# Squares of one half summed on GpSimd, a pair of x splits moved by two steps, and new step times in a hybrid attention trunk

## The chip, the cores and the metric

One core of a Trainium2 chip runs the whole kernel. The time is the device time of one execution in microseconds (us); lower is better. The kernel before takes 2347.12 us, the median of three runs (2345.92 to 2347.37). The profile is of one further execution.

## What is computed

One layer over 1024 positions of width 2048 (`x`, f32). Two groups of eight heads share one input projection; each has q, k, v and a gate.

```python
hn = rmsnorm(h, norm_mix_g);  proj = hn @ w_in          # sb_q..sb_g, df_q..df_g
sb_out = stick_breaking_attention(sb_q, sb_k, sb_v)      # 8 heads of 128
df_out = differential_attention(rope(df_q), rope(df_k), df_v, lam)   # 8 heads, (softmax1 - lam*softmax2) @ v
df_out = rmsnorm(df_out, subln_g) * (1 - lambda_init)
mixed  = concat([sb_out * silu(sb_g), df_out * silu(df_g)])
h = h + mixed @ w_out
gate = sigmoid(rmsnorm(h, norm_ple_g) @ w_ple_gate)
h = h + gate * (p @ w_ple_proj)
return rmsnorm(h, norm_final_g)
```

## The kernel before

Everything lies with the 2048 columns on the partitions (16 tiles of 128) and 512 positions, one half, along the free dimension. A product in f32 is made of three fast ones: each operand is split into a rounded high part (ScalarE, `A.copy` or `A.activation`) and the rest as low part (VectorE, a subtraction), and TensorE does high*high, high*low and low*high. So each operand tile needs a load, a cast on ScalarE and a subtraction on VectorE before TensorE can use it.

The stages, in the order of time in the profile:

1. 0 to 620 us: v and gate columns, with a seven-product (Strassen) scheme, class `Seven`, lines L713 to L715.
2. 620 to 1626 us: 32 units, one for each half and head. A unit (`unit`, L263 to L265) makes q and k of one head from the 16 x tiles in four pieces `pc` of 24 matmuls; beside it the attention of the heads before is interleaved. Half 1 comes first (heads 8 to 15, differential, then 0 to 7, stick-breaking), then half 0 in the same order of heads.
3. 1626 to 1965 us: output projection, again `Seven`. In phase 0 (`ph` 0) six products of each of eight blocks `u` are made for partial results; in phase 1 seven products of 12 matmuls each (A11, A22 of the block before, S2, S4 of the block before, A12, S1, S3) finish a block: four tiles of h, two of each half. `put` stores each tile, and `row_squares` adds its squares to the sum for the next norm.
4. 1965 to 2343 us: gate product, embedding, final norm. `norm` (L2013) turns the sum of squares into the row's scale by a matmul with a matrix of ones.

What sets the order. The five engines run their queues in the order in which the program wrote them; an instruction that waits holds up all behind it on its engine. `Side` is a clock in ticks: one tick for each three matmuls of a unit. A step is entered with a time in ticks, and the instructions are written when the tick comes; fractions only order steps within one tick. The tables at the top of the file are these times: `SC`, `TT` and so on for the differential heads (scores, transposes of the weights), `SBB`, `SBS`, `SBT`, `SGAP` for the stick-breaking ones. `SGAP[0]`, 3.5, is the distance in ticks from `turn` (L484: transposes, then the split L502 on ScalarE and L507 on VectorE) to `mix` (L527 to L532: weights times v) in half 0. Index 0 of a table is half 0, index 1 half 1.

The seam is where unit 15 (half 1, head 7) gives way to unit 16 (half 0, head 8). The x tiles of half 1 are replaced by those of half 0. The last eight come late: `late_x0` loads one (L1352, `xl<-h_d`) and writes its split, `xh` on ScalarE (L1355) and `xl` on VectorE (L1356), `4 + 3 * i` ticks later. In the same ticks VectorE takes q and k of head 7 out of PSUM (L1611), ScalarE casts them (L1619) and VectorE makes their low parts (L1614); the scores of head 7 (L341 to L343) need them.

In phase 1 of the projection the weights of the next blocks are loaded, combined and split while the products run: `diff` (L769) makes T1 to T4 on VectorE from the four loaded blocks, and each load of a next block (L760, `wraw<-w_out`) is issued when the difference that last reads the old block is written, block 21 after T4. `whigh` (L804) casts on ScalarE, `wlow` (L818) subtracts on VectorE. `sums` (L1847 on ScalarE, L1848 to L1856 on VectorE) combines the tiles of h for the gate product. TensorE may add A22 onto the PSUM tile of S3 only when VectorE has read it (L1968, `u3`).

`row_squares` takes the two halves apart. For half 1 ScalarE squares into one buffer, `spare32`, shown as `masks` (L1435), and GpSimd adds it to `total` (L1436). For half 0 ScalarE squares into one of two tiles in turn, `rsq` (L1428), and GpSimd issues a DMA that adds it to one of two tiles in HBM, `sq_d` (L1429; the first two are plain stores). Both `sq_d` tiles are loaded again in the gate stage (L2163), and `norm(*sums0)` makes two matmuls with ones. As one of the `rsq` tiles lies where `cs` lay, the ring of weight buffers of the projection leaves `cs` out: nine buffers in place of ten.

Of the kernel before, what the change touches and what calls it, by code (L numbers as in the profile page):

```python
# [31 lines left out]
EPS = 1e-6  # L32
SUB_EPS = 1e-5

SC = ((6.5, 7, 9.0, 11.5, 15.5, 17.5, 20.0, 21.5), (10.5, 10.5, 15.5, 23.0))
TT = ((19, 31, 16.0), (21.5, 36.5, 20))
DGAP = (3, 7.0)
DF0 = (0.5, 1, 1.5, 3.5, 5.5)
DF1 = (1, 1.0, 3, 5, 6.5)
LV = ((3.0, 4.0), (1, 2))  # L40
LT = ((1, 1.5), (0.5, 2.0))
LM = ((0.5, 2.0, 4, 5), (1.5, 2.5, 4.5, 6.5))
LN = ((1, 6.0), (1, 4.5))
PRIO = 300
NORM_LAT = ((8.0, 8.5), (13, 11))
XLAT = 5
SBB = ((20, 20, 15, 15.5, 16, 16.5, 16.5, 16.0), (19.5, 8.5, 5.0, 3.5, 4.0, 5.5, 5.0, 3.0))
SBS = ((0.5, 3.5, 15.5, 23.5), (-2.5, 3, 7.0, 13.0))
SBT = ((15, 31, 13), (16.0, 30.0, 14.5))
SGAP = (3.5, 6.0)  # L50
SBL = ((1.5, 3, 6.0), (1, 2, 8.0))
SVG = ((18, 37.5, 40, 40, 46), (30.5, 37.5, 41.0, 43.5, 49.5))
CST = (16.5, 19.5)
ROPE = ((-0.4, 1.5, 3.0, 4.0, 2.2, 4.5, 6.0, 7.0), (-1.9, -1, 0, 1, 0.20000000000000018, 2, 3, 4))
ROPE_ = ((3.5, 4.0, 6.0, 10.0, 11.6, 12.5, 15.0), (6.5, 7, 9.5, 12.5, 12.6, 13.5, 14))
VGD = ((19.5, 37, 37.0, 39.5, 44.0), (22.5, 32.5, 35.5, 37.0, 45.0))
LAM0 = 0.8 - 0.6 * math.exp(0.0)
NEG = -1.0e30
EXTRA = 5, 9
PIECES = 30  # L60
LOWG = ORDER1[H - 1:H + 1]
LAST = ((2.5, 3.5), (2, 4.0))
X1T = 1, 2.5, 4, 5.5, 9, 10.5, 12, 13.5
VLAG = 3

# [6 lines left out]
def _body(ctx, nc, tc, ap):  # L72
# [174 lines left out]
    side = Side()  # L247
# [380 lines left out]
    with tc.tile_pool(name="at", bufs=2) as at, ExitStack() as banks:  # L628
# [739 lines left out]
        sq_d = dram.tile([2, P, HALF], F32, name="sq_d", tag="sq_d")  # L1368
        SUMS = "S1", "S2", "S3", "S4"

        def load_operand(ph, nm, i, eng=nc.sync):
# [18 lines left out]
        ssh = {}  # L1390
# [26 lines left out]
        spare32 = masks.bitcast(F32)[:, 0:HALF]  # L1417
        totals = {}

        nsq = [0]  # L1420

        def row_squares(hf, o):
            if hf == 0:
                if nsq[0] % 2:
                    t = at.tile([P, 2, HALF], F32, name="rsq", tag="cs", bufs=1)[:, 0, :]
                else:
                    t = ev.tile([P, HALF], F32, name="rsq", tag="rstd0", bufs=1)
                A.activation(t, o, AF.Square)  # L1428
                G.dma_start(sq_d[nsq[0] % 2], t, **(dict(accum_op=ALU.add) if nsq[0] > 1 else {}))  # L1429
                nsq[0] += 1  # L1430
            elif not totals:
                totals[1] = ev.tile([P, HALF], F32, name="total", tag="rstd1", bufs=1)
                A.activation(totals[1], o, AF.Square)
            else:
                A.activation(spare32, o, AF.Square)  # L1435
                G.tensor_tensor(totals[1], totals[1], spare32, op=ALU.add)  # L1436

        def put(o, ph, hf, ch):

# [80 lines left out]
        for half in (1, 0):  # L1520
# [5 lines left out]
            for hd in (ORDER0, ORDER1)[half]:  # L1526
# [27 lines left out]
                if half == 1 and hd == ORDER1[-1]:  # L1554
                    def late_x0(kt, wait):
                        with tc.issue_after(lastw[0].ins):
                            side.add([(wait, load_x0(kt))])

                    def swap(pc):
                        for i, kt in enumerate((pc * 2, pc * 2 + 8, pc * 2 + 1, pc * 2 + 9)):  # L1560
                            if pc < 2:
                                side.add([(1 + 4 * i, load_x0(kt))])
                            else:
                                side.add([(1 + i, partial(late_x0, kt, 4 + 3 * i))])

                    side.add([(8 * pc + 7, partial(swap, pc)) for pc in range(4)])

# [585 lines left out]
        for u in range(8):  # L2153
            p6(u + 1)
            if u == 0:
                p5(1)
            plew_load(u + 2, 1)
            load_hc(u + 9)
            if u == 5:
                sums0 = [ev.tile([P, HALF], F32, name="sums", tag=t, bufs=1) for t in ("rstd0", "ssq")]  # L2160
                for i, t in enumerate(sums0):
                    with tc.issue_after(op.loaded.ins):
                        nc.sync.dma_start(t, sq_d[i])  # L2163
            if u == 6:
                gate_loads("S3", 0)
            if u == 7:
                embedding_load(0, "xt")
                plew_load(0, 1)
                plew_load(0, 0)
            p3(u)  # L2170
            if u < 7:
                plew(u + 1, 1)
                if u:
                    p5(u + 1)
            if u == 6:
                norm(*sums0)
                ssh[0] = sums0[0]


        hpair = {}  # L2180
# [302 lines left out]
```

## Time and profile before

| | before |
|---|---|
| median of 3 runs | 2347.12 us (2345.92 to 2347.37) |
| the profiled execution, its time | 2344.73 us |
| its span, first to last instruction | 2342.9 us |
| granted TensorE clock, mean | 0.996 |
| TensorE busy | 2300.4 us (98%) |
| VectorE busy | 1828.0 us (78%) |
| ScalarE busy | 1170.5 us (50%) |
| GpSimd busy | 345.4 us (15%) |
| 16 DMA engines, mean rate | 248 GB/s |

How to read it. TensorE works nearly all the time, and the change leaves it almost the same matmuls, so the time can only move by what TensorE waits, by the clock that it is granted, and by the matmuls that go. The view of waits names, for each line, whom it waited for: the sum, how often, and the longest. A timeline row has the start, the duration, and in brackets the idle time of the engine before it and what ended it. The chain of waits goes back from the end of a stretch, at each step to what released it. In the view by stretches the column PEclk is the granted clock. The profiled execution took 2344.73 us, 2.39 us less than the median of the runs.

### The profile page before, as it was taken

The page shows a single profiled execution, that of the slowest core. Times are in us where ns is not written, and L with a number is a line of the kernel's source. Part 1 is how long each engine was busy: PE and PEld are TensorE (multiplying, and loading weights), DVE is VectorE, ACT ScalarE, POOL GpSimd, SP SyncE. Part 2 cuts the span into 40 slices and gives each one's busy share as a digit, 9 for nine tenths or more (in the row PEclk, how much of TensorE's full clock was granted, in tenths as well). Part 3 has the DMA queues.
Part 4 walks back from the last instruction along what each step waited for, and adds up shares of the span by engine and source line. Part 5 has one row for each costly group of instructions (what it writes and reads, how often), then busy time and mean ns, then how long its engine had stood idle before and what let it go on. Part 6 is the DMA issues. An engine that isn't in the chain of part 4 may idle for free.

```text
span 2342.9 us, 32443 instructions
## 1 busy us (share of the span) xinstructions
PE 2300.4 (98%) x10976; PEld 1916.2 (82%) x10976; DVE 1828.0 (78%) x3181; ACT 1170.5 (50%) x2184; POOL 345.4 (15%) x486
## 2 busy tenths in 40 slices
PE   9999999999999999999999999999999999999997
PEld 7888888888888878887888888888888877888886
DVE  7699786777678877777888876668887887788788
ACT  6334243333267776445677765445633335533544
POOL 1211112223200030000001101101111232000000
PEclk9999999999999999999999999999999999999998
DMA  7699579999977788787756666678888778898666
GB/s 254 225 307 354 175 240 288 293 279 265 310 252 252 256 269 314 262 259 245 223 176 189 194 202 208 201 215 244 211 220 217 227 227 278 277 336 290 239 230 218
DMA packets 266549, 581.01 MB, mean 248 GB/s; under 512 B 30032, under 2 KB 58960, under 8 KB 266384
## 3 DMA queue, kind: packets, MB, share of 16 engines
q1 hardware_dynamic: 191776, 394.35, 49.8%
q0 software_dynamic: 55312, 149.71, 24.4%
q10 hardware_dynamic: 19296, 34.90, 4.3%
q8 instruction: 86, 1.41, 0.2%
q14 instruction: 79, 0.65, 0.1%
HBM read 373.32 MB, written 213.91 MB: 251 GB/s over the span
## 4 chain that ended last, share of the span: by engine, by line
PE 76%; DMA 10%; DVE 8%; ACT 4%; issue 1%; SPq 0%; ACTq 0%; DVEq 0%
PE acc L265 8%; PE acc L263 8%; PE acc L264 8%; PE pbc L713 6%; PE pbc L715 6%; PE pbc L714 6%; DMA wlo<-wlo_d 3%; PE pa L714 2%; PE pa L713 2%; PE pa L715 2%; PE tp L484 2%; DMA wraw<-w_gate 2%; DMA wraw<-w_out 2%; PE pb L715 1%; PE pb L713 1%
## 5 line engine op out<-in xcount | busy, mean ns | idle before, releaser
L804 ACT CAST wpr<-T 128x512 fp32r<-128x512 f32 x208 | 125.1, 621 | 484.2 <-DVE T L769 391.6
L263 PE MATMUL acc<-xh,whi 128*128 128x512 f32 x768 | 312.5, 407 | 0.0
L265 PE MATMUL acc<-xh,wlo 128*128 128x512 f32 x768 | 302.0, 393 | 4.7 <-DMA wlo<-wlo_d 4.7
L264 PE MATMUL acc<-xl,whi 128*128 128x512 f32 x768 | 300.9, 392 | 0.0
L265 PEld LDWEIGHTS acc<-xh,wlo 128*128 128x128 f32 x768 | 144.6, 188 | 40.3 <-DMA wlo<-wlo_d 8.5
L264 PEld LDWEIGHTS acc<-xl,whi 128*128 128x128 f32 x768 | 145.4, 189 | 23.7
L263 PEld LDWEIGHTS acc<-xh,whi 128*128 128x128 f32 x768 | 144.9, 189 | 23.6 <-DVE qk L1611 0.3
L804 ACT CAST wpr<-wraw 128x512 fp32r<-128x512 f32 x144 | 88.3, 617 | 140.5 <-DMA wraw<-tw_d 31.3
L818 DVE TENSOR_TENSOR wpr<-T,wpr 128x512 fp32r<-128x512 f32 x208 | 142.5, 685 | 4.7 <-ACT wpr L804 2.1
L946 POOL DMA_DIRECT2D vg_d<-hc x120 | 88.6, 770 | 287.9 <-DVE hc L943 128.9
L502 ACT CAST awh<-tp 128x256 fp32r<-128x256 f32 (+1 forms) x160 | 80.5, 503 | 80.4 <-PE tp L484 74.8
L507 DVE TENSOR_TENSOR awl<-tp,awh 128x256 fp32r<-128x256 f32 (+1 forms) x160 | 92.4, 577 | 35.1 <-ACT awh L502 34.6
L713 PE MATMUL pbc<-cS,wpr 128*128 128x512 f32 x288 | 112.0, 389 | 0.0
L714 PE MATMUL pbc<-cS,wpr 128*128 128x512 f32 x288 | 112.0, 389 | 0.0
L715 PE MATMUL pbc<-cS,wpr 128*128 128x512 f32 x288 | 112.0, 389 | 0.0
L326 DVE CUSTOM_DVE_ANT_0 z<-z,masks 128x512 f32<-128x512 f32 (+7 forms) x128 | 96.9, 767 | 19.0 <-PE z L346 9.8
L818 DVE TENSOR_TENSOR wpr<-wraw,wpr 128x512 fp32r<-128x512 f32 x144 | 97.2, 682 | 11.3 <-ACT wpr L804 11.3
L378 DVE TENSOR_TENSOR_SCAN st<-pt 128x511 f32<-128x511 f32 (+3 forms) x64 | 86.7, 1354 | 23.5 <-ACT pt L371 22.5
L371 ACT ACTIVATE pt<-z 128x512 f32<-128x512 f32 (+3 forms) x64 | 41.7, 652 | 77.3 <-DVE z L354 75.4
L532 PE MATMUL av<-awl,v 128*128 128x256 f32 x256 | 73.0, 285 | 1.2 <-DVE awl L507 1.2
L530 PE MATMUL av<-awh,v 128*128 128x256 f32 x256 | 72.0, 281 | 0.7 <-ACT awh L502 0.7
L531 PE MATMUL av<-awh,v 128*128 128x256 f32 x256 | 72.4, 283 | 0.0
(596 smaller groups left out, 6833.7 us busy)
## 6 DMA issues: line engine op xcount, KB each, us to landing
wlo<-wlo_d SPq DMA_DIRECT2D x94, 512.0 KB, 5.2
whi<-whi_d SPq DMA_DIRECT2D x74, 512.0 KB, 4.1
wraw<-w_vg SPq DMA_DIRECT2D x129, 256.0 KB, 4.2
vg_d<-hc POOLq DMA_DIRECT2D x120, 256.0 KB, 5.5
wraw<-w_in SPq DMA_DIRECT2D x54, 512.0 KB, 5.0
wraw<-w_gate SPq DMA_DIRECT2D x92, 256.0 KB, 5.1
wraw<-w_out SPq DMA_DIRECT2D x72, 256.0 KB, 4.6
wlo_d<-wlo SPq DMA_DIRECT2D x34, 512.0 KB, 3.4
```

What stands on the lines that cost most here:

```text
L263: T.matmul(acc[c], hi[:, k2, kh, c, :], xh, start=first, stop=False)
L264: T.matmul(acc[c], hi[:, k2, kh, c, :], xl, start=False, stop=False)
L265: T.matmul(acc[c], lo[:, k2, kh, c, :], xh, start=False, stop=last)
L326: V.tensor_tensor_reduce(z, z, mwide[:, 0:n], -DF_SCALE, 3.0e38, ALU.add, ALU.min, mx)
L378: V.tensor_tensor_scan(st[:, off + 1:nkey], pt[:, off:nkey - 1], pt[:, off:nkey - 1], initial=1.0, op0=ALU.mult, op1=ALU.bypass)
L507: V.tensor_tensor(wl[:, o, :], tp[:, o, :], wh[:, o, :].bitcast(F32), op=ALU.subtract)
L713: T.matmul(o, wh[:, w], xh, start=start and k == 0, stop=False, skip_group_check=True)
L714: T.matmul(o, wh[:, w], xl, start=False, stop=False, skip_group_check=True)
L715: T.matmul(o, wl[:, w], xh, start=False, stop=k == 3, skip_group_check=True)
L804: A.copy(t[:, 0], src)
L818: V.tensor_tensor(t[:, 1], src, t[:, 0].bitcast(F32), op=ALU.subtract)
L946: G.dma_start(vg_d[hf, blk, u], o, **(dict(accum_op=ALU.add) if ph else {}))
```

## The change

Four things are changed.

The squares of half 0 now go the way of half 1: ScalarE squares into the one buffer `spare32`, GpSimd adds into `totals[0]`. `sq_d`, its 16 storing DMAs and its two loads go, and `norm` gets one tile. The ring of weight buffers of the projection and of the gate stage behind it has `cs` again, ten buffers. `late_x0` writes its splits `6 + 3 * i` ticks after the load instead of `4 + 3 * i`. Some 25 numbers of the tables are others; no step is added or taken away by them.

```diff
-SGAP = (3.5, 6.0)
+SGAP = (4.0, 6.0)
...
 def row_squares(hf, o):
-    if hf == 0:
-        if nsq[0] % 2:
-            t = at.tile([P, 2, HALF], F32, name="rsq", tag="cs", bufs=1)[:, 0, :]
-        else:
-            t = ev.tile([P, HALF], F32, name="rsq", tag="rstd0", bufs=1)
-        A.activation(t, o, AF.Square)
-        G.dma_start(sq_d[nsq[0] % 2], t, **(dict(accum_op=ALU.add) if nsq[0] > 1 else {}))
-        nsq[0] += 1
-    elif not totals:
-        totals[1] = ev.tile([P, HALF], F32, name="total", tag="rstd1", bufs=1)
-        A.activation(totals[1], o, AF.Square)
+    if hf not in totals:
+        totals[hf] = ev.tile([P, HALF], F32, name="total", tag=f"rstd{hf}", bufs=1)
+        A.activation(totals[hf], o, AF.Square)
     else:
         A.activation(spare32, o, AF.Square)
-        G.tensor_tensor(totals[1], totals[1], spare32, op=ALU.add)
+        G.tensor_tensor(totals[hf], totals[hf], spare32, op=ALU.add)
...
-op.ring = [e for e in WRING if e != ("at", "cs")]
...
-                                side.add([(1 + i, partial(late_x0, kt, 4 + 3 * i))])
+                                side.add([(1 + i, partial(late_x0, kt, (6 if pc == 2 else 6) + 3 * i))])
...
-                norm(*sums0)
-                ssh[0] = sums0[0]
+                norm(totals[0])
+                ssh[0] = totals[0]
```

The lines of the new file stand 11 or 12 lower in number behind `row_squares` (L1614 is L1602 there, L1611 is L1599, L1436 is L1425, L1441 is L1430).

VectorE at the seam, before: `xl_9889` is the first late x tile, `q` and `k` are those of head 7.

```order
L507 TENSOR_TENSOR awl<-tp,awh 128x512
L1356 SCALAR_TENSOR_TENSOR xl_9889<-xl_9889,gvec,xh_9888 128x512
L1614 TENSOR_TENSOR q<-qk,q 128x512
L1611 TENSOR_TENSOR qk<-acc_9645,ssa 128x512
L1614 TENSOR_TENSOR k<-qk,k 128x512
L1356 SCALAR_TENSOR_TENSOR xl_9896<-xl_9896,gvec,xh_9895 128x512
```

The same place in the changed kernel:

```order
L507 TENSOR_TENSOR awl<-tp,awh 128x512
L1602 TENSOR_TENSOR q<-qk,q 128x512
L1599 TENSOR_TENSOR qk<-acc_9644,ssa 128x512
L1356 SCALAR_TENSOR_TENSOR xl_9889<-xl_9889,gvec,xh_9888 128x512
L1602 TENSOR_TENSOR k<-qk,k 128x512
L542 TENSOR_REDUCE sm<-av 128x128
L544 TENSOR_TENSOR sg<-sm,sg 128x256
L1356 SCALAR_TENSOR_TENSOR xl_9895<-xl_9895,gvec,xh_9894 128x512
```

The low part of q and the reading of k out of PSUM now stand ahead of the first late x tile; the low part of k still stands behind it. On ScalarE the first late `xh` stays where it was, between the casts of q and k.

GpSimd in one block of phase 1 of the projection, before: `h_d` is the store of a tile of h, `hq` and `hc` are such tiles.

```order
L1436 TENSOR_TENSOR total<-total,masks 128x512
L1441 DMA h_d<-hq 128x512
L1429 DMA sq_d<-rsq 128x512
L1441 DMA h_d<-hc 128x512
L1429 DMA sq_d<-rsq 128x512
L1441 DMA h_d<-hc 128x512
```

The same block in the changed kernel:

```order
L1425 TENSOR_TENSOR total<-total,masks 128x512
L1430 DMA h_d<-hq 128x512
L1425 TENSOR_TENSOR total<-total,masks 128x512
L1430 DMA h_d<-hc 128x512
L1425 TENSOR_TENSOR total<-total,masks 128x512
L1430 DMA h_d<-hc 128x512
```

Two DMAs of each block have become two additions in the same places; the order on ScalarE and VectorE is the same there.

TensorE at the first products of the output projection, while head 7 of half 0 is still in its attention, before: these rows stand some matmuls behind the transposes L484 of one `turn`, and L530 begins its `mix`.

```order
L713 MATMUL pa<-cA11h,wfhi 128x512
L714 MATMUL pa<-cA11l,wfhi 128x512
L715 MATMUL pa<-cA11h,wflo 128x512
L530 MATMUL av<-awh,v 128x256
L531 MATMUL av<-awh,v 128x256
L532 MATMUL av<-awl,v 128x256
```

The same place in the changed kernel:

```order
L713 MATMUL pa<-cA11h,wfhi 128x512
L714 MATMUL pa<-cA11l,wfhi 128x512
L715 MATMUL pa<-cA11h,wflo 128x512
L339 MATMUL z<-k,q 128x256 x2
L341 MATMUL z<-k_15418,q 128x512
L342 MATMUL z<-k_15418,q 128x512
L343 MATMUL z<-k_15418,q 128x512
L530 MATMUL av<-awh,v 128x256
```

From the transposes to L530 stood nine matmuls of the projection; now stand twelve, and the five of a later score.

More of the change, by code (lines that the diff above doesn't have):

```diff
@@ L33 @@
 SUB_EPS = 1e-5
-SC = ((6.5, 7, 9.0, 11.5, 15.5, 17.5, 20.0, 21.5), (10.5, 10.5, 15.5, 23.0))
-TT = ((19, 31, 16.0), (21.5, 36.5, 20))
+SC = ((7.0, 8.5, 9.0, 11.5, 15.5, 17.5, 21.0, 21.5), (10.5, 10.5, 15.5, 23.0))
+TT = ((19, 31, 17.0), (21.5, 36.5, 20))
 DGAP = (3, 7.0)
@@ L39 @@
 DF1 = (1, 1.0, 3, 5, 6.5)
[L40 to L43, printed above, removed]
+LV = ((1.0, 5.5), (1, 2))
+LT = ((1, 2.0), (0.5, 2.0))
+LM = ((0.5, 2.0, 4, 6.0), (1.5, 2.5, 4.5, 6.5))
+LN = ((1, 3.0), (1, 4.5))
 PRIO = 300
-NORM_LAT = ((8.0, 8.5), (13, 11))
+NORM_LAT = ((11.0, 8.5), (13, 11))
 XLAT = 5
-SBB = ((20, 20, 15, 15.5, 16, 16.5, 16.5, 16.0), (19.5, 8.5, 5.0, 3.5, 4.0, 5.5, 5.0, 3.0))
-SBS = ((0.5, 3.5, 15.5, 23.5), (-2.5, 3, 7.0, 13.0))
+SBB = ((20, 20, 16.5, 15.5, 16, 16.5, 16.5, 16.0), (19.5, 8.5, 5.0, 3.5, 4.0, 5.5, 5.0, 3.0))
+SBS = ((0.5, 3.5, 15.5, 23.0), (-2.5, 3, 7.0, 11.0))
 SBT = ((15, 31, 13), (16.0, 30.0, 14.5))
-SGAP = (3.5, 6.0)
[L51 to L54, printed above, removed]
+SGAP = (4.0, 6.0)
+SBL = ((1.5, 3, 6.0), (1.5, 2, 8.0))
+SVG = ((18, 37.5, 40, 40, 45.5), (30.5, 37.5, 40.0, 42.5, 48.5))
+CST = (17.5, 19.5)
+ROPE = ((-1.9, 1.5, 3.0, 4.0, 2.2, 4.5, 6.0, 7.0), (-1.9, -1, 0, 1, 0.20000000000000018, 2, 3, 4))
 ROPE_ = ((3.5, 4.0, 6.0, 10.0, 11.6, 12.5, 15.0), (6.5, 7, 9.5, 12.5, 12.6, 13.5, 14))
-VGD = ((19.5, 37, 37.0, 39.5, 44.0), (22.5, 32.5, 35.5, 37.0, 45.0))
+VGD = ((19.5, 37.5, 37.5, 40.0, 44.5), (22.5, 32.5, 35.5, 37.0, 45.0))
 LAM0 = 0.8 - 0.6 * math.exp(0.0)
@@ L61 @@
 LOWG = ORDER1[H - 1:H + 1]
-LAST = ((2.5, 3.5), (2, 4.0))
+LAST = ((2.0, 3.0), (2, 4.0))
 X1T = 1, 2.5, 4, 5.5, 9, 10.5, 12, 13.5
@@ L1367, in _body @@
         q_d = dram.tile([8, 2, P, HALF], F32, name="q_d", tag="q_d")
-        sq_d = dram.tile([2, P, HALF], F32, name="sq_d", tag="sq_d")
         SUMS = "S1", "S2", "S3", "S4"
@@ L2158, in _body @@
             load_hc(u + 9)
[L2159 to L2163, printed above, removed]
             if u == 6:
```

1 line of the change is left out of this document (removed).

## Prediction

> **What bounds the kernel now.** I read the page first, then the waits of TensorE, then timelines, the chain of waits and stretches at the two places where the longest of those waits lie.
>
> ```profile
> span 2342.9 us, 32443 instructions
> PE 2300.4 (98%) x10976; PEld 1916.2 (82%) x10976; DVE 1828.0 (78%) x3181; ACT 1170.5 (50%) x2184; POOL 345.4 (15%) x486
> ...
> PE pbc L713 <- DVE u L1968: 5.2, 5, 1.9
> PE acc L265 <- DMA wlo<-wlo_d: 4.7, 8, 1.1
> PE z L341 <- ACT k L1619: 2.2, 1, 2.2
> ...
> PE av L532 <- DVE awl L507: 1.2, 4, 0.4
> ...
> PE av L527 <- DVE lead L506: 1.0, 1, 1.0
> ...
> PE z L345 <- ACT k L1681: 0.9, 1, 0.9
> ...
> PE av L530 <- ACT awh L502: 0.7, 1, 0.7
> ```
>
> TensorE is idle for 2342.9 - 2300.4 = 42.5 us of the span. The change takes two matmul rows from it and adds none, so it can gain only from those waits, from the clock behind them, and from the two. Of the waits, L265 on `wlo` is a load that the change does not touch; the others listed lie where it moves something. All sums are made on the profiled execution (2344.73 us), which is 2.39 us under the median of the runs (2347.12); the differences are carried over to that median.
>
> **The seam: the splits of x, two ticks later.** Rows of TensorE, ScalarE and VectorE at the end of unit 15, and the load of the first late x tile from the chain of waits:
>
> ```profile
> 1066.28 0.49 PE L484 MATMUL tp<-ident,bt 128*128 128x128 f32 x3
> 1069.01 0.49 PE L341 MATMUL z<-k,q 128*128 128x512 f32 x1 [2.24 <-ACT k L1619]
> 1069.74 0.50 PE L342 MATMUL z<-k,q 128*128 128x512 f32 x1 [0.23 <-DVE k L1614]
> ...
> 1070.36 0.63 PE L263 MATMUL acc<-xh,whi 128*128 128x512 f32 x1
> ```
> ```profile
> 1065.60 0.72 ACT L1355 ACTIVATE xh<-xl,gvec 128x512 fp32r<-128x512 f32 x1 [3.62 <-DMA xl<-h_d]
> 1068.34 0.62 ACT L1619 CAST k<-qk 128x512 fp32r<-128x512 f32 x1 [2.02 <-DVE qk L1611]
> ```
> ```profile
> 1066.35 0.75 DVE L1356 SCALAR_TENSOR_TENSOR xl<-xl,gvec,xh 128x512 fp32r<-128x512 f32 x1 [3.50 <-ACT xh L1355]
> 1067.02 0.68 DVE L1614 TENSOR_TENSOR q<-qk,q 128x512 fp32r<-128x512 f32 x1
> 1067.62 0.68 DVE L1611 TENSOR_TENSOR qk<-acc,ssa 128x512 f32<-128x512 f32 x1
> 1068.99 0.69 DVE L1614 TENSOR_TENSOR k<-qk,k 128x512 fp32r<-128x512 f32 x1 [0.69 <-ACT k L1619]
> ```
> ```profile
> 1057.66 7.91 DMA xl<-h_d
> ```
>
> The load ends at 1057.66 + 7.91 = 1065.57. ScalarE waits for it, VectorE's `xl` waits for that, and behind it stand q's low part and the reading of k, neither of which needs x: L1611 starts at 1067.62, the cast at 1068.34, L341 at 1069.01. In the new order both stand ahead of `xl`, where VectorE had 3.50 us of nothing. The cast of k still stands behind `xh` on ScalarE, so the load still sets it: `xh` 1065.60, cast some 0.65 later (rows of an engine overlap by 0.1), 1066.25, L341 0.67 after the cast's start as before, 1066.9. k's low part now comes behind `xl` (1066.35), so at about 1067.0, and L342 0.75 after that, 1067.7 to 1067.8. From L342 to the next L263 stay 0.62: 1068.4 instead of 1070.36, a gain of **2.0**. Since the load's end is fixed, what is gained ahead of it (the 0.98 at L527, also moved) only becomes a longer wait here; I cost it and the other steps of unit 15 at nothing, covered by this load. If the load came earlier too, they would be worth up to 1.0.
>
> Behind that gap the clock falls, which the same two stretches show, and again behind another gap in the projection:
>
> ```profile
> 1066.28:1070.36 4.08, 1.61 (x8) 0.93 (x7) 3.32 (x6) 1.88 (x6) 0.38 (x1) 0.98 1.08 356
> 1070.36:1073.95 3.59, 3.59 (x11) 2.83 (x9) 3.41 (x9) 2.31 (x4) 0.15 (x1) 0.54 0.88 241
> ```
> ```profile
> 1902.95 0.69 PE L713 MATMUL pbc<-cA,wpr 128*128 128x512 f32 x1 [1.88 <-DVE u L1968]
> ...
> 1906.70 0.39 PE L713 MATMUL pbc<-cA,wpr 128*128 128x512 f32 x1
> 1906.93 0.40 PE L714 MATMUL pbc<-cA,wpr 128*128 128x512 f32 x1
> ```
>
> The granted clock is 0.54 in the 3.59 us after the seam's gap. In the projection the nine matmuls from 1902.95 take 3.75 us; at the pace of the last two rows (1906.93 - 1906.70 = 0.23) they would take 2.07, so a fall costs **1.7**. The shortest gap with a fall that I quote is 1.88. At the seam the gaps left are 1066.9 - 1066.7 and some 0.4 at L342; the fall should go, so the seam gives 2.0 + 1.7 = **3.7**. The Trainium skill, "TensorE: Matmul & The Clock Gate", Part 1, has the half rate come only after an idle window of some 3.4 us; by that page neither gap would cost any clock, the seam would give 2.0 alone and the projection 2.5: -5.65 in all. The measured 0.54 behind a gap of 2.24 decides against it.
>
> What could hold that back is the next load in line:
>
> ```profile
> 1069.54 0.38 SPq L185 DMA_DIRECT2D wlo<-wlo_d  x1
> ```
> ```profile
> wlo<-wlo_d SPq DMA_DIRECT2D x1, 512.0 KB, 8.6
> ```
> ```profile
> 1082.08 0.39 PE L265 MATMUL acc<-xh,wlo 128*128 128x512 f32 x1
> ```
>
> It lands at 1069.54 + 8.6 = 1078.1 and is used at 1082.08, so TensorE can move ahead by 3.9 before this wait appears: just enough for 3.7.
>
> **Other moved steps.** The tables put the first score of head 8 one tick later (three matmuls of 0.23, 0.7 us), which covers most of the 0.9 at L345: **0.7**. `SGAP[0]` and the places around it put each `mix` of half 0 one tick, or as in the quoted order three matmuls and a score, behind where it stood; the waits of L530 (0.7) and L532 (1.2) for the split behind `turn` are 0.7 or less each, and most are in half 0: **1.3** of 1.9, between 0 and 1.9. Against it, each of some 25 new places can meet an instruction that isn't ready. No row shows which; the kind is that of L532, 1.2 / 4 = 0.3 each, and I take five of them: **+1.5** (0 to 4).
>
> **The squares.** In phase 1 TensorE waits five times for L1968. The chain of waits over three blocks, cut to one round, and before it the issues of the same load in a stretch of phase 0 (12, 256 KB, median):
>
> ```profile
> wraw<-w_out SPq DMA_DIRECT2D x12, 256.0 KB, 4.0
> ```
> ```profile
> 1876.55 1.28 DVE hq L1848
> ...
> 1882.97 1.67 DVE hc L1856
> ...
> 1889.15 0.61 DVE T L769
> ...
> 1889.81 6.08 DMA wraw<-w_out
> ...
> 1897.77 1.28 DVE hq L1848
> ```
>
> It is a ring: L1848, VectorE's work down to T4 (L769), the load that T4 lets go, ScalarE's cast and squares, L1848 again, in 1897.77 - 1876.55 = 21.2 us. TensorE's own block is 7 x 12 matmuls of 0.23, 19.1 to 19.3. The ring is longer, so TensorE waits. What the change does to it has two signs. GpSimd's rows:
>
> ```profile
> 1882.26 1.83 POOL L1436 TENSOR_TENSOR total<-total,masks 128x512 f32<-128x512 f32 x1 [2.25 <-ACT masks L1435]
> ...
> 1888.65 0.90 POOL L1429 DMA_DIRECT2D sq_d<-rsq  x1 [1.82 <-ACT rsq L1428]
> ...
> 1891.23 0.86 POOL L1429 DMA_DIRECT2D sq_d<-rsq  x1 [1.12 <-ACT rsq L1428]
> ...
> 1897.20 1.29 POOL L1436 TENSOR_TENSOR total<-total,masks 128x512 f32<-128x512 f32 x1 [3.47 <-ACT masks L1435]
> ```
>
> The two accumulating stores run in the very stretch of the load, which takes 6.08 here and 4.0 in phase 0, where there are none. Without them the load is between 0 and 2.1 shorter; the stores of `h_d` stay, so I take half, 1.0. On the other side two additions of 1.29 to 1.83 come in their place. Beside an addition VectorE's L1848 takes 1.28 (1897.77, the addition from 1897.20), and L1856 1.67 (1882.97, the addition from 1882.26), against 0.75 for the same kind and size at L1356: 0.5 to 0.9 is lost for each that it meets. The first new one starts when the store did, 1888.65, and T4 comes at 1889.15: 0.5 lost. The second falls at 1891.2, while the ring waits for the load: nothing lost. So a round is 0.5 shorter, and the five waits shrink by 5 x 0.5 = 2.5. The one of 1.88 becomes 1.4, and with it I count the fall of the clock as gone, 1.7; as that threshold is seen only from above, and the waits of less than 0.5 can't give all of it, I take **3.5** of 4.2 (from 6.9, all of 5.2 and 1.7, down to a loss, below).
>
> The Trainium skill, "SBUF — State Buffer", section "SBUF: two separate sides", speaks against this change: VectorE and GpSimd share a pair of ports as an exclusive lock, an operation of VectorE with two inputs in SBUF and one of GpSimd shut each other out for the whole instruction. By that page each new addition can cost VectorE a full 1.29; the rows of 1.28 and 1.67 agree in kind, with 0.5 to 0.9.
>
> ScalarE now squares four times a block into one buffer and must wait until GpSimd has read it; GpSimd's additions lie 2.6 us apart (1888.65, 1891.23) and take 1.29, so it waits for nothing, and without that distance it would cost ScalarE, half idle, a microsecond. The tenth buffer of the ring costs nothing and gives nothing: what bounds is the load behind T4.
>
> The norm of the gate stage makes one product for half 0 in place of two:
>
> ```profile
> 2203.77 1.88 PE L2013 MATMUL ssps<-sums,onesr 128*128 128x512 f32 x4
> 2205.08 0.80 PE L2000 MATMUL pc<-cgS4h,wpr 128*128 128x512 f32 x1
> ```
>
> Four passes take 1.31, two 0.65: **0.65** gained. The two loads of `sq_d` that go were waited for by nobody on this list.
>
> The sum: -3.7 - 0.7 - 1.3 + 1.5 - 3.5 - 0.65 = -8.35. Against the median: 2347.12 - 8.35 = **2338.8** (a profiled execution of 2336.4). A measurement tells some 0.2% (4.7 us) from no change: faster is under 2342.4, slower over 2351.8.
>
> **The rivals.** First, slower: the ring grows. If both additions meet VectorE on the ring, at the 0.92 that L1856 lost, and the load is limited by its own 16 engines and not by the squares, a round is 1.84 longer. Over six rounds that is +11.0, and with the other terms (-3.7 - 0.7 - 1.3 + 1.5 - 0.65 = -4.85) +6.2: 2353.3. It decides from (4.85 + 4.7) / 6 = 1.6 per round. By the lock that the Trainium skill states ("SBUF — State Buffer", above) a round could lose 2 x 1.29, for 2357.8. For it: the rows of 1.28 and 1.67 and a GpSimd that works in the same stretch. Against: only the addition by T4 lies on the ring. Chance 0.08.
>
> Second, the gains are hidden by loads. The stretch of the seam has a DMA share of 1.08, so the x tile, or the `wlo` with its 0.2 us to spare, may come later, and the gap stays long enough for the half clock; and the load in the projection doesn't get shorter, its 1.0 set against 0.5. Then the seam gives 2.0, the projection 0: -2.0 - 0.7 - 1.3 + 1.5 - 0.65 = -3.15, 2344.0, no change that can be told. For it: that share. Against: the squares are the main traffic that phase 1 has over phase 0. Chance 0.15.
>
> Third, the new places bring as many waits as they take (+4 in place of +1.5, L530 and L532 as before): -8.35 + 2.5 + 1.3 = -4.55, 2342.6, on the border. Chance 0.08.
>
> **How the numbers follow.** The forecast has 0.69. Its own lower end takes all the waits and the clock of phase 1 (6.9), all of 1.9, and no new waits: -3.7 - 0.7 - 1.9 - 6.9 - 0.65 = -13.85, 2333.3. The upper end is the second rival with 1 us more for its unknown waits, 2345.0; above it lies the first rival. Faster: 0.69 + half of the third rival, less a little for the upper part of the forecast's own range, 0.72. Slower 0.08. Same 0.20.
>
> **What would show it.** In the profile after, L341 at the end of unit 15 waits under 0.5, no stretch behind it has a clock near 0.5, and L1611 of k starts ahead of `xl`. The loads behind T4 take about 5 us, the sum of TensorE's waits for L1968 is under 3, and L769 beside an addition takes up to 0.5 longer. L2013 has two passes there. I am wrong if the waits for L1968 have grown, if the gap at the seam is still near 2, or if new waits of attention sum to over 3.

## The result, and the profile after

The changed kernel takes 2334.5 us (median of 6 runs, 2331.7 to 2336.96) against 2346.78 for the kernel before in the same comparison (6 runs, 2345.32 to 2348.71). The ratio is 0.995, with a 95% interval of 0.9939 to 0.9961: 11.7 us faster, between 9 and 14. The forecast was 8.35 less, with 2338.8 as the time: the direction and the order of size are right, 3 us of the gain are not in it, and the time lies 1.2 us above the lower end of the stated range (2333.3). Below, a ratio r is turned into (1 - r) x 2347 us.

The page and the waits of TensorE in the changed kernel, in the order of those of before. Behind the colon stand the sum in us, how often, and the longest:

```profile
span 2332.4 us, 32435 instructions
PE 2296.1 (98%) x10974; PEld 1915.0 (82%) x10974; DVE 1838.4 (79%) x3181; ACT 1170.8 (50%) x2184; POOL 354.4 (15%) x485
```
```profile
PE acc L265 <- DMA wlo<-wlo_d: 4.5, 9, 1.0
PE pbc L713 <- ACT masks L1424: 1.9, 1, 1.9
...
PE pbc L713 <- DVE hq L1962: 1.3, 1, 1.3
...
PE z L341 <- ACT k L1607: 0.9, 1, 0.9
...
PE av L527 <- DVE lead L506: 0.5, 1, 0.5
...
PE z L345 <- ACT k L1669: 0.2, 1, 0.2
PE pbc L713 <- DVE u L1956: 0.2, 1, 0.2
```

The idle time of TensorE went from 42.5 to 36.3 us and its busy time from 2300.4 to 2296.1: two passes fewer in the norm are 0.86 of that (1.88 us for four before, 1.02 for two now), the rest is matmuls that no longer run at half clock. Between the start and the last stage no half clock is left. The waits for u3 (L1968 before, L1956 now) were 5.2 in all; under that name 0.2 is left. But the wait of 1.9 at the end of phase 1, which the view puts down to ScalarE's `masks`, is one more of them. It stands where TensorE adds A22 onto S3 of the last block, and TensorE starts right behind VectorE's L1956, whose row is the first here:

```profile
1949.68 0.68 DVE L1956 TENSOR_TENSOR u<-pbc,s 128x512 f32<-128x512 f32 x1
```
```profile
1950.50 0.47 PE L713 MATMUL pbc<-cA,wpr 128*128 128x512 f32 x1 [1.89 <-ACT masks L1424]
```

L1956 ends at 1950.36. In the kernel before TensorE starts at this place just as far, 0.14 to 0.15 us, behind the end of L1968, with hardly a wait, though ScalarE's last instruction had ended 1.5 us earlier. So the waits for u3 went from 5.2 to 2.1 (the prediction's sign had them under 3), and the 1.3 for L1962, which is also VectorE's, was 0.2.

The seam, rows of TensorE, ScalarE and VectorE, with the load of the first late x tile from the chain of waits, and the stretch behind it:

```profile
1066.50 0.50 PE L341 MATMUL z<-k,q 128*128 128x512 f32 x1 [0.89 <-ACT k L1607]
1067.38 0.50 PE L342 MATMUL z<-k,q 128*128 128x512 f32 x1 [0.38 <-DVE k L1602]
...
1067.95 0.39 PE L263 MATMUL acc<-xh,whi 128*128 128x512 f32 x1
```
```profile
1065.22 0.72 ACT L1355 ACTIVATE xh<-xl,gvec 128x512 fp32r<-128x512 f32 x1 [4.95 <-DMA xl<-h_d]
1065.85 0.60 ACT L1607 CAST k<-qk 128x512 fp32r<-128x512 f32 x1
```
```profile
1061.67 0.69 DVE L1599 TENSOR_TENSOR qk<-acc,ssa 128x512 f32<-128x512 f32 x1
1065.97 0.75 DVE L1356 SCALAR_TENSOR_TENSOR xl<-xl,gvec,xh 128x512 fp32r<-128x512 f32 x1 [3.62 <-ACT xh L1355]
1066.64 0.69 DVE L1602 TENSOR_TENSOR k<-qk,k 128x512 fp32r<-128x512 f32 x1
```
```profile
1057.19 8.01 DMA xl<-h_d
```
```profile
1067.95:1071.50 3.55, 3.55 (x18) 3.02 (x17) 3.41 (x7) 2.31 (x4) 1.17 (x2) 1.00 1.04 331
```

L1599 of k now runs at 1061.67, long before the load lands (1057.19 + 8.01 = 1065.20). The cast of k stands directly behind `xh` and still waits for that load; L263 comes at 1067.95 in place of 1070.36, and the granted clock behind it (the column after the fifth engine) is 1.00 where it was 0.54.

The chain of waits over two rounds of phase 1. It holds no DMA:

```profile
1867.94 1.38 DVE hq L1836
...
1880.69 0.28 DVE T L769
1880.97 0.79 issue
...
1883.68 1.79 DVE wpr L818
1885.47 0.61 DVE hc L1857
...
1886.70 0.72 ACT hq L1835
...
1887.45 1.61 DVE hq L1836
```

One round is 1887.45 - 1867.94 = 19.5 us, against 21.2 before and 19.1 to 19.3 of TensorE's own. The load behind T4 in this round, and GpSimd's and VectorE's rows beside it:

```profile
wraw<-w_out SPq DMA_DIRECT2D x1, 256.0 KB, 2.8
```
```profile
1879.98 1.30 POOL L1425 TENSOR_TENSOR total<-total,masks 128x512 f32<-128x512 f32 x1 [1.67 <-ACT masks L1424]
...
1883.11 1.81 POOL L1425 TENSOR_TENSOR total<-total,masks 128x512 f32<-128x512 f32 x1 [1.31 <-ACT masks L1424]
```
```profile
1880.61 1.23 DVE L769 TENSOR_TENSOR T<-wraw,T 128x512 f32<-128x512 f32 x1
...
1883.68 1.79 DVE L818 TENSOR_TENSOR wpr<-T,wpr 128x512 fp32r<-128x512 f32 x1
```

The load takes 2.8 us where it took 6.08, so it is off the path altogether. Both new additions meet VectorE: T4 (L769) takes 1.23 in place of 0.68, L818 1.79 in place of 0.68. Busy time by engine over the same 80 us, before and after (the third figure in brackets is VectorE):

```profile
1860.00:1940.00 80.00, 76.10 (x325) 61.54 (x324) 62.83 (x92) 28.81 (x52) 27.34 (x31) 0.98 0.77 226
```
```profile
1860.00:1940.00 80.00, 79.81 (x352) 65.55 (x351) 75.64 (x99) 30.86 (x55) 34.91 (x33) 1.00 0.66 224
```

TensorE is busy for 79.81 of 80; VectorE went from 62.83 to 75.64. Before, it waited for ScalarE, which stood behind the load; now it is nearly full.

### The profile page after: what moved, and what is told of

Read it like the earlier page. It is cut to its first block, busy times and chain, and to the rows that moved or that the text cites. A ratio compares the mean times of both kernels' runs of the same rounds, so it can differ in the third digit from the quotient of the medians.

```text
span 2332.4 us, 32435 instructions
## 1 busy us (share of the span) xinstructions
PE 2296.1 (98%) x10974; PEld 1915.0 (82%) x10974; DVE 1838.4 (79%) x3181; ACT 1170.8 (50%) x2184; POOL 354.4 (15%) x485
## 4 chain that ended last, share of the span: by engine, by line
PE 80%; DVE 8%; DMA 7%; ACT 3%; issue 2%; SPq 0%; ACTq 0%; DVEq 0%
PE acc L265 8%; PE acc L263 8%; PE acc L264 8%; PE pbc L713 6%; PE pbc L714 6%; PE pbc L715 6%; DMA wlo<-wlo_d 3%; PE pa L715 2%; PE pa L714 2%; PE pa L713 2%; PE tp L484 2%; PE pb L1990 1%; PE pb L714 1%; PE pb L713 1%; PE pb L715 1%
## 5 line engine op out<-in xcount | busy, mean ns | idle before, releaser
L263 PE MATMUL acc<-xh,whi 128*128 128x512 f32 x768 | 311.8, 406 | 0.0
L263 PEld LDWEIGHTS acc<-xh,whi 128*128 128x128 f32 x768 | 144.6, 188 | 23.5 <-DVE qk L1599 0.3
L818 DVE TENSOR_TENSOR wpr<-T,wpr 128x512 fp32r<-128x512 f32 x208 | 150.8, 725 | 4.3 <-ACT wpr L804 1.4
L713 PE MATMUL pbc<-cS,wpr 128*128 128x512 f32 x288 | 112.0, 389 | 0.0
L818 DVE TENSOR_TENSOR wpr<-wraw,wpr 128x512 fp32r<-128x512 f32 x144 | 97.6, 686 | 10.5 <-ACT wpr L804 9.2
L530 PE MATMUL av<-awh,v 128*128 128x256 f32 x256 | 72.0, 281 | 0.5 <-ACT awh L502 0.5
```

Of the source, the lines that this page charges most:

```text
L263: T.matmul(acc[c], hi[:, k2, kh, c, :], xh, start=first, stop=False)
L713: T.matmul(o, wh[:, w], xh, start=start and k == 0, stop=False, skip_group_check=True)
L818: V.tensor_tensor(t[:, 1], src, t[:, 0].bitcast(F32), op=ALU.subtract)
```

## The experiments

The theory after the traces: the seam's gain is the gap and the half clock behind it; the squares' gain is the difference between a load that comes back sooner and additions that hold VectorE; the tables give what they take from the waits in attention. Rivals: the tenth buffer of the ring is the cause; the additions eat up the gain; the parts hang on each other.

Besides whole times, stages are compared within traces: from the first L713 of the projection to the first norm (phase 0 and 1), and from unit 15 to unit 17 (the seam). Whole times of the kernel before spread from 2341.6 to 2352.9 in these comparisons, the stages less. How much less can be seen in the projection: the seam alone and the tables alone, below, leave phase 1 as it was before, and both take 366.1 in the projection, where the trace of before has 368.0 (the tables shorten its start by some 1.5). In that trace a half clock fell in the projection (1903.09), in those two none. So 2 us between two single traces of this stage can be chance, and differences from 368.0 are also given from 366.1.

**The squares alone.** All of the squares' edits, old seam and tables.

```diff
 def row_squares(hf, o):
-    if hf == 0:
...
-        G.dma_start(sq_d[nsq[0] % 2], t, **(dict(accum_op=ALU.add) if nsq[0] > 1 else {}))
...
+    if hf not in totals:
...
+        G.tensor_tensor(totals[hf], totals[hf], spare32, op=ALU.add)
...
-op.ring = [e for e in WRING if e != ("at", "cs")]
```

> The squares' part alone (half 0 added by GpSimd, no sq_d, ring of ten, one tile to the norm), everything else as before. Theory: the loads behind T4 fall from about 6 to about 3 us, the ring becomes VectorE's own, 19.5 us a round in place of 21.2, and the waits for u3 and the half clock behind them go: about 6 us up to the first norm and 0.65 at the second, -6.5 against before. The prediction on record: -4.15 (3.5 + 0.65). Rival (the new additions take back what the load gives): 0 to -2.

Ratio 0.9971 (0.996 to 0.9982): -6.8 us. In its trace the projection takes 1992.57 - 1629.12 = 363.5, before 1995.01 - 1626.97 = 368.0, after 1984.83 - 1622.71 = 362.1. The whole is as the theory said; the projection is 4.5 shorter than in the trace of before and 2.6 than 366.1, where the theory had 6.

**The ring left at nine.** As above, with one line kept:

```diff
+op.ring = [e for e in WRING if e != ("at", "cs")]
```

> As the squares' part alone, but the ring of weight buffers is left at nine. Theory (the missing stores do it): the same as with ten buffers within 1 us, -6.5. Rival (the tenth buffer lets loads start earlier and is the cause): at most half of the gain is left, -3 or less, and the loads behind T4 are short but VectorE or ScalarE waits for buffers.

Ratio 0.9968 (0.9955 to 0.998): -7.5 us, projection 363.0. The tenth buffer gives nothing that shows, and at least half of the gain is there without it: that rival is out.

**The seam alone.**

```diff
-partial(late_x0, kt, 4 + 3 * i)
+partial(late_x0, kt, (6 if pc == 2 else 6) + 3 * i)
```

> Only the splits of x two ticks later, with the old tables and squares. Theory: L341 at the end of unit 15 waits under 1 us in place of 2.24, the next score's L263 starts 2 us earlier, and no half clock follows: -3.7 against before. Rival (the clock does not hang on this gap, or the wlo load behind takes it back): -2.0 or less.

Ratio 0.9982 (0.9973 to 0.9991): -4.2 us. TensorE at the seam of this kernel, where no half clock follows:

```profile
1066.62 0.49 PE L341 MATMUL z<-k,q 128*128 128x512 f32 x1 [0.23 <-ACT k L1619]
...
1068.07 0.39 PE L263 MATMUL acc<-xh,whi 128*128 128x512 f32 x1
```

Units 15 and 16 together take 56.2 us, before 59.4: 3.2 less. Counted from the start of unit 15 (1034.43, before 1034.78), 1.9 of that is gained up to this L263 and 1.3 behind it.

**The tables alone.**

```diff
-SGAP = (3.5, 6.0)
+SGAP = (4.0, 6.0)
...
-SC = ((6.5, 7, 9.0, 11.5, 15.5, 17.5, 20.0, 21.5), (10.5, 10.5, 15.5, 23.0))
+SC = ((7.0, 8.5, 9.0, 11.5, 15.5, 17.5, 21.0, 21.5), (10.5, 10.5, 15.5, 23.0))
```

> Only the 25 numbers of the tables, with the old seam and squares. The prediction on record sums to -0.7 - 1.3 + 1.5 = -0.5. From the trace after: units 27 to 31 are 1.1 shorter, unit 17 is 0.2 longer, units 18 to 26 0.2 shorter, unit 10 0.25 shorter: -1.3. Rival (the tables are what made the seam or the projection start better): -3 or more.

Ratio 0.9985 (0.9973 to 0.9996): -3.5 us, so nearer to the rival's number than to the theory's, though with an interval of 3 us either way. Of the rival's two reasons the seam isn't one: its units 15 and 16 take 59.6, as before. The start of the projection is: its first 480 product matmuls take 134.2, before 135.7. What the tables give is said below, from all the traces together.

**What the stores and the additions cost, each by itself.** Four kernels: the accumulating stores left out of before; all those stores plain; the additions and the old stores together; the changed kernel without half 0's additions.

```diff
-G.dma_start(sq_d[nsq[0] % 2], t, **(dict(accum_op=ALU.add) if nsq[0] > 1 else {}))
+if nsq[0] < 2:
+    G.dma_start(sq_d[nsq[0] % 2], t)
```

> Before, with the 14 accumulating stores of the squares of half 0 left out (the two first plain stores stay, so the sum for the second norm lacks the rest). No new additions. Theory (traffic of those stores makes the load behind T4 long): the loads behind T4 fall to 3 us, the waits for u3 go, -6 or a little more, since VectorE meets fewer additions. Rival (something else in the squares' part): loads stay near 6 us and the time near 0.

```diff
-G.dma_start(sq_d[nsq[0] % 2], t, **(dict(accum_op=ALU.add) if nsq[0] > 1 else {}))
+G.dma_start(sq_d[nsq[0] % 2], t)
```

> Before, with every store of the squares plain in place of accumulating (each overwrites the last, so the sum lacks the rest). The same bytes go out of SBUF. Theory A (any store of 256 KB beside the load lengthens it): loads behind T4 stay at 5 us or more, time within 1.5 us of before. Theory B (accumulating is the costly form): loads fall to about 4 us or under, time -4 to -6.

```diff
 G.tensor_tensor(totals[hf], totals[hf], spare32, op=ALU.add)
+if hf == 0:
+    G.dma_start(sq_d[nsq[0] % 2], o, **(dict(accum_op=ALU.add) if nsq[0] > 1 else {}))
+    nsq[0] += 1
```

> The squares' part, and beside it the old accumulating stores kept (of the tile of h itself, read by nothing): both costs at once. Theory (two signs, the load and the additions): loads behind T4 near 6 us again, VectorE's additions beside it, T4 later by 0.5: +2 to +6 against before, the first rival of the prediction at its price. Rival (additions cost nothing on the ring): within 1 us of before less 0.65.

```diff
-G.tensor_tensor(totals[hf], totals[hf], spare32, op=ALU.add)
+if hf:
+    G.tensor_tensor(totals[hf], totals[hf], spare32, op=ALU.add)
```

> The changed kernel with half 0's additions left out (the squares are still made, but the second norm sees only the first). Theory: VectorE's L818, L1836 and L1857 around the new additions lose their extra time (1.79 to 0.69, 1.38 to 0.75), VectorE is no longer 96% busy in phase 1; TensorE hardly waited there, so the time is only 0 to 2 us under that of the changed kernel, from the 1.9 and 1.3 of waits at the end of phase 1. Rival (the additions still hold the ring and with it TensorE): 4 us or more under it.

Their times, and from one trace of each the projection (first L713 to the first norm) and the load behind T4 in the four rounds from 1860 us on:

| kernel | stores of the squares | half 0 added | ratio to before (95%) | projection, us | load behind T4, us |
|---|---|---|---|---|---|
| before | accumulating | no | 1 | 368.0 | 5.5 to 6.2 |
| additions and old stores | accumulating | yes | 1.0007 (0.9994 to 1.002) | 371.7 | 4.9 to 5.9 |
| plain stores | plain | no | 0.9962 (0.9948 to 0.9976) | 361.6 | 4.1 to 4.4 |
| squares alone | none | yes | 0.9971 (0.996 to 0.9982) | 363.5 | 2.6 to 3.0 |
| changed kernel | none | yes | 0.995 (0.9939 to 0.9961) | 362.1 | 2.7 to 3.0 |
| accumulating stores left out | two plain | no | 0.9941 (0.9926 to 0.9956) | 359.0 | 3.0 to 3.3 |
| changed, half 0 not added | none | no | 0.9919 (0.9904 to 0.9934) | 357.2 | 3.0 to 3.8 |

The load follows the stores: longest beside the accumulating ones, between with plain ones, short without. So the plain stores went as theory B said, only with more gain, 8.9 in place of 4 to 6. With the accumulating ones left out the whole time is 13.8 less, where 6 or a little more was expected; the projection has at most 9.0 of it, and where the rest lies isn't known.

The first, second, fourth and sixth row are two by two. The stores cost 368.0 - 359.0 = 9.0 without the additions and 371.7 - 363.5 = 8.2 with them. The additions cost 371.7 - 368.0 = 3.7 with the stores and 363.5 - 359.0 = 4.5 without; the changed kernel loses 362.1 - 357.2 = 4.9 by them. From 366.1 the first of these is 7.1 and the third 5.6. The whole times are too coarse for this: by the ratios, each with some 3 us of interval, the stores cost 13.8 and 8.4, the additions 1.6 and 7.0. So the two signs of the prediction are both there, each larger than it said. The wait of TensorE for u3 with both at once, 5.2 in the kernel before:

```profile
PE pbc L713 <- DVE u L1961: 7.7, 6, 2.3
```

The whole time of that kernel isn't told from before; in the projection it loses 3.7 to 5.6, within what the theory gave, though the profiled execution is the slowest of its ten (2353.72, median 2349.32).

The stretch of phase 1 without half 0's additions, VectorE at 71.69 in place of 75.64:

```profile
1860.00:1940.00 80.00, 80.00 (x355) 66.27 (x354) 71.69 (x103) 31.21 (x56) 21.32 (x26) 1.00 0.69 231
```

There TensorE waits for nothing, and the 1.9 and 1.3 at the end of phase 1 are gone too. I had put this kernel at 0 to 2 us under the changed one; it is 7 under by the ratios, 4 by the medians and 4.9 in the projection, so the rival was nearer. The changed kernel's waits for VectorE there, 1.9, 1.3 and 0.2, are 3.4 of the 4.9; the rest lies earlier in the projection and wasn't followed further.

**The seam and the tables, each undone.** The changed kernel with the splits back at 4 ticks, and with the old tables.

```diff
-partial(late_x0, kt, (6 if pc == 2 else 6) + 3 * i)
+partial(late_x0, kt, 4 + 3 * i)
```

> The changed kernel with the splits of x put back to 4 ticks. Theory: L341 at the end of unit 15 waits 2 to 3 us again, and a half clock of 3.4 us follows, so 3 to 4 us of the changed kernel's gain of 12 are lost: about -8.5 against before. Rival (with the new tables the seam is no longer late): within 1 us of the changed kernel, -11 or more.

Ratio 0.9963 (0.9949 to 0.9977): -8.7 us, 3.0 short of the changed kernel; units 15 and 16 take 59.5, after 56.7. The gap and the half pace are back (rows of TensorE):

```profile
1069.00 0.72 PE L341 MATMUL z<-k,q 128*128 128x512 f32 x1 [3.02 <-ACT k L1607]
...
1070.74 0.63 PE L263 MATMUL acc<-xh,whi 128*128 128x512 f32 x1
```

The second puts all of these tables back to those of before:

```diff
-SGAP = (4.0, 6.0)
+SGAP = (3.5, 6.0)
...
```

> The changed kernel with the old tables: squares and seam alone. Theory: the parts add up, -6.8 (squares alone) and -4.2 (seam alone): -11, so that the tables are worth 1 or less in this company. Rival (the tables' own -3.5 is real and adds): -8.5, 3.5 short of the changed kernel.

Ratio 0.9962 (0.9948 to 0.9976): -8.9 us, 2.8 short of the changed kernel. So the tables look worth some 3 us in either company, nearer to the rival; between two ratios with some 3 us of interval each that isn't settled, and the stages below give 2.4. The three parts alone sum to -4.2 - 6.8 - 3.5 = -14.5, the change is -11.7: with these intervals that doesn't show that the parts hang on each other, nor that they don't.

**A version that avoids both costs.** Half 0's squares aren't made in the projection at all. The second norm needs them only some 200 us later, and GpSimd is nearly idle in between. The tiles are loaded again from `h_d`, one for each step of the gate stage, squared and added there.

```diff
 def row_squares(hf, o):
+    if hf == 0:
+        return
...
+def late_square():
+    n = len(sq0)
+    if n and sq0[-1] is not None:
+        t = sq0[-1]
+        if n == 1:
+            totals[0] = ev.tile([P, HALF], F32, name="total", tag="rstd0", bufs=1)
+            A.activation(totals[0], t, AF.Square)
+        else:
+            A.activation(t, t, AF.Square)
+            G.tensor_tensor(totals[0], totals[0], t, op=ALU.add)
+    if n < 16:
+        if n % 2 == 0:
+            late[0] = at.tile([P, 2, HALF], F32, name="hsq", tag="cs", bufs=1) if n == 0 else late[0]
+        t = late[0][:, n % 2, :]
+        nc.sync.dma_start(t, h_d[0, n])
+        sq0.append(t)
+    else:
+        sq0.append(None)
```

> A version meant to beat both: the changed kernel, but the squares of half 0 are not made in the projection at all; the sixteen tiles of half 0 are loaded again in the gate stage (4 MB more), squared by ScalarE and added by GpSimd there, one tile behind each of seventeen steps, through the two halves of cs (ring of nine). Theory (the additions cost because VectorE is full in the projection; in the gate stage TensorE waits for nothing): the time of the kernel without half 0's additions, -19 against before, give or take 2 for the sixteen loads. Rival (the gate stage is as full, its DMA share is 0.9 to 1.0): -12 or worse, with TensorE waiting for weights in the gate stage.

Ratio 0.9956 (0.9941 to 0.9972): -10.3 us, no better than the change. The projection takes 358.1, as hoped. From there to the second norm it is 211.3 (208.7 after): TensorE waits 2.29 for weights whose load took 6.22 us beside the first loads of squares, and a half clock follows:

```profile
2089.38 0.50 PE L1993 MATMUL pb<-cgS,wpr 128*128 128x512 f32 x1 [2.29 <-DVE wpr L818]
...
2091.05 0.63 PE L1993 MATMUL pb<-cgS,wpr 128*128 128x512 f32 x1
```

That the squares' loads held up the other is argued from this. Only the places of the loads are changed in the next one, three in each block from the second on:

```diff
 load_hc(u + 2)
-if u > 2:
-    late_square()
...
 p6(u + 1)
-if u < 6:
+if 0 < u < 7:
     late_square()
...
```

> The version meant to beat both, once more: as the late squares, but the sixteen loads come some 40 to 50 us later in the gate stage, three for each block from the second S2 block on, where the DMA share of the changed kernel is 0.65 to 0.9 in place of 0.9 to 1.0. Theory (the 4 us lost at 2079 to 2094 came from loads of weights that the squares' loads held up): no wait over 0.7 us in the gate stage and no half clock there, 4 us less than with the first places: -14 to -16 against before. Rival (any sixteen loads in this stage delay the weights): -10 again, with the wait at another place.

Ratio 0.9935 (0.9921 to 0.9949): -15.3 us, median 2332.56, the lowest here of a kernel that leaves nothing out. Its projection takes 357.9, and from there to the second norm 207.1 (208.7 after). A wait of 1.2 is left just behind that norm, where under 0.7 was expected:

```profile
PE pc L1991 <- DVE hc L2152: 1.2, 1, 1.2
```

Against before its whole interval lies under 1. Against the change it is some 2 to 4 us faster by the medians and ratios, but in different comparisons and with intervals that overlap, so that isn't shown. That moving the loads took the wait of 2.29 away fits the argument.

## Why the prediction was right, point by point

Of the 3.35 us that the forecast lacks, the tables have most, 1.9 by the stages and up to 3 by the ratios. The other terms come out near their sums, the squares' partly by two errors that make up for each other.

**The seam: -3.7; measured -4.2 alone, -3.0 when undone, by the stage 3.2 and 2.8.** The steps held: L1599 and the low part of q ahead of `xl`, the load still setting the cast, L341 at 1066.50 (forecast 1066.9), L342 at 1067.38 (1067.7), L263 at 1067.95 (1068.4), and no fall of the clock. L263 is 2.4 earlier, but unit 15 had begun 0.45 earlier (1034.33), so 1.96 of it is the seam's, the 2.0 of the forecast. The clock behind it gave 1.3 in the seam alone and not 1.7. L341 was to wait under 0.5; in the changed kernel it waits 0.89, since TensorE came there sooner, as the step on the fixed load said (in the seam alone it waits 0.23). What the sum left out is a new wait of 0.55 for L527 at 1086.49. It stands in the four traces that have both the later splits and the new tables, and in none of the others; it lay under the five new waits of the list.

```profile
1086.49 0.51 PE L527 MATMUL av<-lead,v 128*128 128x256 f32 x2 [0.55 <-DVE lead L506]
...
1097.98 0.50 PE L345 MATMUL z<-k,q 128*128 128x512 f32 x1 [0.21 <-ACT k L1669]
...
1102.33 0.44 PE L345 MATMUL z<-k,q 128*128 128x384 f32 x1 [0.30 <-ACT et L402]
```

**The tables: -0.7 - 1.3 + 1.5 = -0.5; measured about -3.** The step that was mis-sized is the +1.5 of new waits. From unit 17 to the projection TensorE's waits without those for `wlo` sum to 1.5 to 1.8 in the eight traces with the old tables and to 0.4 to 0.5 in the six with the new ones: 1.2 less, new waits included, and the only new one there is some 0.3 at L345. The waits for `wlo` themselves, 4.2 to 8.0 by trace, differ more from run to run than by kernel. Taken a little further, from unit 17 to 480 product matmuls into the projection, beside which head 7 ends, and less those waits, the median trace is 664.1 with the old and 662.0 with the new tables (663.7 to 667.8, and 661.4 to 663.7), 2.1 less, the 1.2 among it; the other 0.9 isn't put down to any wait. Units 0 to 14 are 0.3 shorter (medians 415.3 and 415.0). Together that is 2.4 of some 3. L345 went from 0.90 to 0.21, but 0.30 came back at its next score.

**The squares in the projection: -3.5; measured -4.5 (368.0 to 363.5) or, from 366.1, -2.6; in the changed kernel -5.9 or -4.0, with about 1 of it the tables' (134.7 in place of 135.7 for its first 480 matmuls).** The mechanism is right and both its sizes are too small; that the net came out near is in part luck, since the one error makes up for the other. The relief of the load was put at 1.0 a round, half of what separates 6.08 from the 4.0 of phase 0; it is 3, since the load takes 2.8 without the stores, less than in phase 0. That made the load no longer the end of the ring, so most of its relief can't be used. The additions were put at 0.5 a round, at T4 alone (it lost 0.55, 1.23 against 0.68); the second was covered "while the ring waits for the load". That cover went with the load: it now meets L818, and 1.1 is lost there. The two by two gives 7.1 to 9.0 for the stores and 3.7 to 5.6 for the additions, where the prediction had 6.7 (5 x 1.0 and the clock) and 2.5.

**The half clock.** It went at both places. That the length of a gap decides, as the prediction took it, is wrong: the last section shows falls behind 1.66 and none behind 2.85. In the changed kernel the gap of 1.89 at the end of phase 1 had none, and the seam alone had none in the projection with the old stores. So the 1.7 that the prediction counts there is chance, and at the seam a fall cost less than 1.7, as the last section shows.

**The norm: -0.65.** Two passes in place of four:

```profile
2193.50 1.02 PE L2001 MATMUL ssps<-total,onesr 128*128 128x512 f32 x2
...
2194.88 0.40 PE L1989 MATMUL pc<-cgS4l,wpr 128*128 128x512 f32 x1
```

From the first pass to the second matmul behind the norm it is 2194.88 - 2193.50 = 1.38; the same two rows stood at 2203.77 and 2205.72 before, 1.95: 0.57 less.

**The rivals.** The first, both additions on the ring and no relief, was built: the kernel with additions and old stores loses 3.7 to 5.6 in the projection, 0.6 to 0.9 a round and not 1.84, so even this doesn't reach the 1.6 from which it decides. The second failed at both of its places: the load behind T4 got shorter, and the `wlo` of unit 16 wasn't late at 1078.1 (no wait there in the trace after). The third failed: the new places brought less than they took.

## What to carry to other kernels

When a transfer ends a loop, ask what else runs in its stretch and in which form: taking 14 accumulating stores out of the way of a load of the same size was worth 7 to 9 us, and about half of that was paid back because the work moved onto an engine that the shorter loop then filled. When a cover is "the engine waits there anyway", it goes with the very wait that the change removes. An addition that no one needs for 200 us needn't be made where the engines are full, but where its loads are placed matters: with the same sixteen loads the whole change came to 10 or to 15 us.

## What the runs showed of the hardware

An accumulating store costs more than its bytes. The stores of squares in a stretch of phase 1 of the kernel before, and the same, plain, with the loads beside them:

```profile
wraw<-w_out SPq DMA_DIRECT2D x12, 256.0 KB, 3.8
sq_d<-rsq POOLq DMA_DIRECT2D x8, 256.0 KB, 5.6
```
```profile
wraw<-w_out SPq DMA_DIRECT2D x12, 256.0 KB, 3.7
sq_d<-rsq POOLq DMA_DIRECT2D x8, 256.0 KB, 3.8
```

By the medians they land 1.8 us sooner, and the projection goes from 368.0 (or 366.1) to 361.6: of the 7.1 to 9.0 that the stores cost, 4.4 to 6.4 are the form and 2.6 the bytes, in one trace of each.

The clock falls to half for 3.41 us behind some gaps of TensorE, but not by a threshold of their length. In the fourteen traces, between the start and the last stage, 29 gaps are longer than 1.65 us, and behind 16 of them it fell. The shortest with a fall is 1.66, in the squares alone; the longest without is 2.85, at the seam of the kernel with additions and old stores, while all seven other seams with the old splits (2.24 to 3.03) had a fall. Behind 1.88 it fell in the kernel before, behind 1.89 it didn't in the changed one. Of the shorter gaps, 1.50 to 1.65, none was followed by a fall. The two extremes, with the next matmuls at 0.63 and at 0.40:

```profile
1421.51 0.50 PE L265 MATMUL acc<-xh,wlo 128*128 128x512 f32 x1 [1.66 <-DMA wlo<-wlo_d]
...
1422.22 0.63 PE L264 MATMUL acc<-xl,whi 128*128 128x512 f32 x1
```
```profile
1069.04 0.49 PE L341 MATMUL z<-k,q 128*128 128x512 f32 x1 [2.85 <-ACT k L1612]
...
1070.33 0.40 PE L263 MATMUL acc<-xh,whi 128*128 128x512 f32 x1
```

What decides stands in the traces' records of the granted clock. In each of the ten traces that have more than one, all starts of a half clock lie whole multiples of 3.4133 us apart, to 0.01 us, also the longer one of the last stage: in the kernel before they are 1070.24, 1903.09 and 2329.76, that is 244 and then 125 of them. So the clock goes by windows of this length, and where their borders fall differs from trace to trace. Counted by these windows, TensorE's idle time sorts the cases: with 2.14 us or more in one window a half clock followed at its end in all 11 cases, with 1.63 or less in none, and between them in 5 of 11. The gap of 2.85 lay across a border, with 1.90 in one window.

So a gap of 1.7 to 3 us costs a fall or not by where it lies, which the program doesn't set, and one that shrinks below 1.6 had none here. A fall doesn't always cost the 1.7 of the projection: from L341 to unit 17 it is 24.0 us in the three traces without a fall and without the wait at L527, and 24.8 to 25.2 in the seven with one, so 0.8 to 1.2. The Trainium skill, "TensorE: Matmul & The Clock Gate", Part 1, calls the window that is watched free-running, so that the moment of a gap would count and not its length alone; these starts agree with that, but the 3.4 us of idleness that it asks for are more than any window here had before a fall (1.66 to 3.02).
